# Two changes of order in an fp32 two-block transformer kernel: matmuls of rounded weights ahead of those of the remainders, and the next weights converted behind token tile 0's norm

## The chip, the core and the metric

The kernel runs on one core of one Trainium2 chip. The core has a matrix engine (TensorE, PE in the rows; its weight loads are listed apart as PEld), VectorE (DVE), ScalarE (ACT), GpSimd (POOL) and queues that start transfers (SyncE's is SP). The metric is the device time of one launch in microseconds, the median of several runs.

## The reference, cut to what matters

256 tokens of width 1024 pass through two transformer blocks. The first has stick-breaking attention beside a short convolution, then a gated feed-forward network with a convolution; the second has a gated delta rule (GDN) beside a forgetting attention (fox), then a squared-ReLU feed-forward network. Around them stand norms and residuals. At the end of the first block's mixing, and on into its feed-forward network, the reference reads:

```python
def rms_norm(x, g):
    xf = x.astype(jnp.float32)
    var = jnp.mean(xf * xf, axis=-1, keepdims=True)
    return (xf * lax.rsqrt(var + RMS_EPS) * g.astype(jnp.float32)).astype(x.dtype)
...
        x = x + rms_norm(merged @ w_out[l], norm_mix_post[l])

        h = rms_norm(x, norm_ffn_pre[l])
        u = causal_dwconv(h @ w_up[l], conv_ffn_w[l])
        a, g = jnp.split(u, 2, axis=-1)
        f = (jax.nn.gelu(g, approximate=True) * a) @ w_down[l]
        x = x + rms_norm(f, norm_ffn_post[l])
...
        hn = rmsnorm(h, norm_mlp_g[l])
        x = h + jnp.square(jax.nn.relu(hn @ w_up[l])) @ w_down[l]
```

All operands are fp32.

## The kernel before

**Products of split numbers.** A matrix product in fp32 is made of three products of rounded parts. A weight piece w (a `raw` tile of 512 KB, brought in by SP) is rounded by a cast on ScalarE to `wh`, and VectorE subtracts to get the remainder `wl`; this pair of instructions is `convert` of the class `Wt`, and stands in the trace at L183 and L184. Activations are split in the same way by `split` (cast on ScalarE, L122; subtraction on VectorE, L125). The raw tiles go round in 4 buffers, the `wh` tiles in 5 and the `wl` tiles in 4. The product is hi·hi + hi·lo + lo·hi.

**Two forms.** `mm_T` keeps weights in the array and moves activations: for each of 8 slices k of the contraction, `wh` meets [hi | lo] of 256 tokens (512 columns, L224), and then `wl` meets hi (256 columns, L225); 16 matmuls fill one tile `pT`. The text calls the two the wide and the narrow matmul. ScalarE and VectorE then read `pT`. `mm_N` keeps activations of one token tile (128 tokens, `tt` is 0 or 1) in the array and moves weights, always 512 columns (L261 to L263). Most projections go by `mm_T`; the output and down-projections (tiles `pN`) and the first projections of a stage go by `mm_N` (tiles `pM`).

**Transitions.** Between a projection that ends a stage and the next stage stand, for each token tile, `post_norm` (squares of the product on ScalarE, `fg` and `x` on VectorE), `norm` (two squares on ScalarE, the chain of small operations of `rsqrt` on VectorE, then `xm`), and `to_T` (eight transposes on TensorE into `tr`, then four splits). `normed` writes them for both tiles, with tile 0's transposes ahead of tile 1's norm. `head_N` (and `head_T`, which calls it) loads the first weights of the next stage, two `Wt` of four pieces each, and multiplies tile 0 by both, then tile 1. `down_tail` ends a projection: tile 0 finishes first, so that its norm runs beside tile 1's matmuls. There are four such places: in front of the first block's mixing (without `normed`), from the first output projection to the up-projection (near 195 us), from the down-projection to the second block (near 400 us), and from the second output projection to the last up-projection (near 745 us).

**What sets the order.** The code is written in one stream; a scheduler puts each engine's instructions in an order by its own estimate of when their inputs are there. Each engine works through its list strictly, and waits at its head.

Of the kernel before, what the change touches and what calls it, by code (L numbers as in the profile page):

```python
# [14 lines left out]
AF = mybir.ActivationFunctionType  # L15
ALU = mybir.AluOpType
AX = mybir.AxisListType

P = 128
T = 256  # L20
NT = T // P
D = 1024
KD = D // P
# [16 lines left out]
def two_blocks(ctx, tc, ins, out):  # L40
    nc = tc.nc
# [45 lines left out]
    mm = nc.tensor.matmul  # L87

    class Act:
# [3 lines left out]
        def __init__(self, s, n=KD, per=2, alloc=None):  # L93
            self.s, self.per, self.alloc, self.hl = s, per, alloc or t4, []
            for _ in range(0, n, per):
                self.more()
# [22 lines left out]

    def split(hi, lo, src, eng=None):  # L120
        if eng is None:
            nc.scalar.copy(hi, src)  # L122
        else:
            eng.tensor_copy(hi, src)
        nc.vector.tensor_sub(lo, src, hi)  # L125

    nc.scalar.preload_act_table_set("natural_log_exp_and_others")

# [31 lines left out]
    class Wt:  # L160


        def __init__(self, w, k0, n, c0, cols, alloc=None, later=False, raws=None):
            self.k0, self.per = k0, max(1, 1024 // cols)
            self.pieces, self.raw = [], []
            for k in range(k0, k0 + n, self.per):
                m = min(self.per, k0 + n - k)
                raw = wp.tile([P, m, cols], F32, tag="raw", name=nm("raw"), bufs=4) if raws is None else \
                    raws("raw", (P, m, cols))
                nc.sync.dma_start(raw, w[k * P:(k + m) * P, c0:c0 + cols].rearrange("(k p) c -> p k c", p=P))  # L170
                if alloc is None:
                    wh = wp.tile([P, m, cols], F32R, tag="wh", name=nm("wh"), bufs=5)
                    wl = wp.tile([P, m, cols], F32R, tag="wl", name=nm("wl"))
                else:
                    wh, wl = alloc("wh", (P, m, cols), F32R), alloc("wl", (P, m, cols), F32R)
                self.pieces.append((wh, wl))
                self.raw.append(raw)
                if not later:
                    self.convert()

        def convert(self):
# [36 lines left out]
    def mm_T(dst, wt, ct, kt, x):  # L218


        cs = slice(ct * P, (ct + 1) * P)
        for k in range(kt):
            wh, wl = wt.at(k, cs)
            mm(dst, wh, x.both(k), start=(k == 0), stop=False, skip_group_check=True)  # L224
            mm(dst[:, T:2 * T], wl, x.at(k)[0], start=False, stop=(k == kt - 1), skip_group_check=True)  # L225

    def proj_T(w, c0, ncols, x, dst=None):

# [46 lines left out]
    def tail_weights(w, k0, k1, alloc=None):  # L275
        return [Wt(w, k, 1, 0, D, alloc) for k in range(k0, k1)]

    def down_tail(banks, w, parts, wts, first):

        m = len(wts)  # L280
        wts = wts + tail_weights(w, parts[m][0], parts[-1][0] + 1)
        both = list(zip(wts, parts))
        for tt in range(NT):
            order = [(n, q) for q in both[:m] for n in range(2)] if tt == 0 else [(0, q) for q in both[:m]]
            order += [(0, q) for q in both[m:]]
            order += [(1, q) for q in (both[m:] if tt == 0 else both)]
            for n, (wt, (k, x, xk)) in order:
                mm_N(banks[tt][n], wt, k, x, xk, tt, slice(n * 512, (n + 1) * 512),
                     first and k == parts[0][0], k == parts[-1][0])

    def head_N(w, cols, x, ready, done):


        wts = [Wt(w, 0, KD, c, 512, a) for c, a in zip(cols, (tc4, None))]
        for tt in range(NT):
            ready(tt)
            for n in (0, 1) if tt == 0 else (1, 0):
                pt = pj("pM")
                for k in range(KD):
                    mm_N(pt, wts[n], k, x, k, tt, slice(None), k == 0, k == KD - 1)  # L300
                done(n, tt, pt)

    def head_T(w, cols, x, ready):

        nat = [t4("nat", (P, NT, 512)) for _ in cols]

        def done(n, tt, pt):
            nc.scalar.copy(nat[n][:, tt, :], pt)

        head_N(w, cols, x, ready, done)  # L310

        def pairs(t):
            for j in (0, 2):
                pt = pj("pT", (P, 2, T))
                for i in range(2):
                    for tt in range(NT):
                        nc.tensor.transpose(pt[:, i, tt * P:(tt + 1) * P], t[:, tt, (j + i) * P:(j + i + 1) * P], ident)
                yield j, pt

        return [pairs(t) for t in nat]  # L320


    def rsqrt(ss, scale, eps=EPS):


        v = nc.vector
        terms = ss if isinstance(ss, list) else [ss]
        shape = list(terms[0].shape)
        r, rc, q, y = tn("rsr", shape), tn("rsc", shape), tn("rsq", shape), tn("rsy", shape)
        for t in terms:  # L330
            a = tn("rsa", shape)
            if isinstance(eps, float):
                v.tensor_scalar(a, t, scale, eps, ALU.mult, ALU.add)
            else:
                v.scalar_tensor_tensor(a, t, scale, eps, ALU.mult, ALU.add)
            eps = a
        v.tensor_scalar(r.bitcast(I32), a.bitcast(I32), -0.5, float(0x5F300000), ALU.mult, ALU.add)
        v.tensor_mul(q, r, r)
        v.tensor_scalar(rc, r, -0.3985661334391346, None, ALU.mult)
        v.tensor_mul(y, q, a)  # L340
        v.scalar_tensor_tensor(q, y, -3.921194022600673, y, ALU.add, ALU.mult)
        v.scalar_tensor_tensor(q, q, 6.097508583838679, y, ALU.add, ALU.mult)
        v.scalar_tensor_tensor(r, q, -5.685303430259191, rc, ALU.add, ALU.mult)
        return r

    def norm(x, tt, g):

        s2 = tn("ss2", (P, 2))
        sq = t2("sq")
        for n in range(2):  # L350
            nc.scalar.activation(sq, x[tt][:, n * 512:(n + 1) * 512], AF.Square, accum_out=s2[:, n:n + 1])
        r = rsqrt([s2[:, 0:1], s2[:, 1:2]], 1.0 / D)
        xm = t4("xm", (P, D))
        for q in range(2):
            cs = slice(q * 512, (q + 1) * 512)
            gq = g[q] if isinstance(g, list) else g[:, cs]
            nc.vector.scalar_tensor_tensor(xm[:, cs], x[tt][:, cs], r, gq, ALU.mult, ALU.mult)
        return xm

    def to_T(dst, tt, xm, eng=None):  # L360

        for q in range(2):
            pt = pj("tr", (P, 4, P))
            for i in range(4):
                k = q * 4 + i
                nc.tensor.transpose(pt[:, i, :], xm[:, k * P:(k + 1) * P], ident)
            for i in (0, 2):
                split(*dst.at(q * 4 + i, slice(tt * P, (tt + 1) * P), 2), pt[:, i:i + 2, :], eng)

    def normed(x, g, dst, mid):  # L370

        xms = []
        for tt in range(NT):
            mid(tt)
            xms.append(norm(x, tt, g))
            if tt == 0:
                to_T(dst, 0, xms[0])
        return lambda tt: to_T(dst, tt, xms[tt]) if tt else None

    def post_norm(x, tt, banks, g):  # L380

# [14 lines left out]
    xr = [t4("x", (P, D)) for _ in range(NT)]  # L396
    nc.sync.dma_start(xr[0], x_in[0:P, :])
    g = t4("gain", (P, D))
# [5 lines left out]
            nc.sync.dma_start(xr[1], x_in[P:T, :])  # L404
    h = Act("hT")
    for tt in range(NT):
        to_T(h, tt, norm(xr, tt, g))
    for w in wv:
        w.convert()
    vN = t4("vN", (P, NT, ATT_W))  # L410
# [49 lines left out]
    pt = ps("pc")  # L460
    nc.tensor.transpose(pt[:, 0:g0 + 3], prow, ident[0:g0 + 3, 0:g0 + 3])
    nc.vector.tensor_copy(pcol, pt[:, 0:g0 + 3])
    pt = ps("fc")
# [107 lines left out]
    for j, pt in proj_T(w_in, CB, CONV_W, h):  # L571
        y = t2("cby", (P, 2, T))
# [36 lines left out]

    banks = proj_full_N(ins["w_out"][0], mh)  # L610
    ready = normed(xr, g_pre, h2, lambda tt: post_norm(xr, tt, banks[tt], g_post))


    w_up, w_down = ins["w_up"][0], ins["w_down"][0]
# [10 lines left out]
    banks = [[ps("pN"), ps("pN")] for _ in range(NT)]  # L625
    parts, first = [], True
# [20 lines left out]
    for (j, pa_), (_, pg_) in zip(*gens):  # L647
        if j >= 4:
            flush(NFH - 1)
        if j == NFH - 2:  # L650
            wts = tail_weights(w_down, NFH - TAIL, NFH - 4, tc4)
        y = []
        for part, pt in enumerate((pa_, pg_)):
            yy = t2("yy", (P, 2, T))
            for i in range(2):
                c = part * NFH + j + i
# [12 lines left out]
    ready = normed(xr, g_pre, u, lambda tt: post_norm(xr, tt, banks[tt], g_post))  # L669
# [493 lines left out]
    for j in range(0, KD, 2):  # L1163
        y = oTa[j // HG][:, j % HG:j % HG + 2, :]
# [4 lines left out]
    for j, pt in proj_T(ins["w_proj_gdn_2"][0], 0, D, ga):  # L1169
        y = t2("my", (P, 2, T))  # L1170
        nc.vector.scalar_tensor_tensor(y, sa[j // 4][:, j % 4:j % 4 + 2, :], 1.0, pt, ALU.add, ALU.mult)
        nc.vector.tensor_add(y, y, mb[j // 4][:, j % 4:j % 4 + 2, :])
        hi, lo = mh.at(j, n=2)
# [3 lines left out]
    hn = Act("hnT")  # L1177

    banks = proj_full_N(ins["w_out_2"][0], mh)

    xr = [t4("x", (P, D)) for _ in range(NT)]
# [8 lines left out]
    ready = normed(xr, g_mlp, hn, add_mix)  # L1190


    w_up, w_down = ins["w_up_2"][0], ins["w_down_2"][0]
    NK = D_FF_2 // P
    heads = head_T(w_up, (0, 512), hn, ready)
    head = chain(heads[0], ((4 + j, pt) for j, pt in heads[1]))
    gen = mix(head, (1, 3, 5, 7), 8, proj_T(w_up, 1024, D_FF_2 - 1024, hn))
    banks = [[ps("pN"), ps("pN")] for _ in range(NT)]
    parts, tails, first = [], [], True
    for j, pt in gen:  # L1200
# [6 lines left out]
        fh, o = ffn_act(j, NK - 1)  # L1207
        split(*fh.at(o, n=2), y)
        parts += [(j + i, fh, o + i) for i in range(2)]
    down_tail(banks, w_down, parts, wts, False)  # L1210
    for tt in range(NT):
        yo = t4("yo", (P, D))
        for n in range(2):
# [27 lines left out]
```

## Time and profile before

| | |
|---|---|
| median of 3 runs | 937.69 us (937.58 to 938.1) |
| the profiled execution | 936.81 us |
| its span, first to last instruction | 935.1 us |
| mean granted TensorE clock in it | 0.996 of 2.4 GHz |
| busy: TensorE, VectorE, ScalarE, GpSimd | 97%, 71%, 61%, 8% |

An engine's busy share is the share of the span in which at least one of its instructions runs. Matmuls overlap in the array, so a duration of one is longer than what it adds to the time; the distance between starts tells that. The granted clock is the share of full speed that the chip gave TensorE.

### The profile page before, as it was taken

How to read it: one execution, taken by the hardware profiler on the slowest of the kernel's cores; microseconds unless marked ns; L12 is line 12 of the kernel's file. 1: busy time of each engine (PE TensorE's matmuls, PEld its weight loads, DVE VectorE, ACT ScalarE, POOL GpSimd, SP SyncE). 2: the span in 40 equal slices, each digit the busy share in tenths (PEclk: the TensorE clock that was granted, in tenths of full speed). 3: DMA queues.
4: the chain of work that ended last, by engine and by line, in shares of the span. 5: the costliest groups of instructions: out<-in, count | busy, mean ns of one | idle time of the engine just before them, and what ended most of it. 6: DMA issues, size and time to landing. Idle time of an engine off the chain costs nothing.

```text
span 935.1 us, 13379 instructions
## 1 busy us (share of the span) xinstructions
PE 909.5 (97%) x4871; PEld 762.0 (81%) x4871; DVE 663.4 (71%) x1164; ACT 572.6 (61%) x987; POOL 74.9 (8%) x127
## 2 busy tenths in 40 slices
PE   5999999989999999999999999999999999999998
PEld 4887888768888888778888778888988778888886
DVE  6567657884888789867989878645688765555553
ACT  5567756554766666657867667754456456556561
POOL 4000000000000000000000089602000000000000
PEclk9999999989999999999999999999999999999999
DMA  7743456654564655564554354544346654556542
GB/s 252 227 139 113 130 186 226 203 180 139 180 201 159 208 174 199 197 210 128 163 160 128 100 157 145 159 136 138 100 135 226 222 181 159 187 176 198 181 151 99
DMA packets 118858, 157.87 MB, mean 169 GB/s; under 512 B 9813, under 2 KB 96072, under 8 KB 118792
## 3 DMA queue, kind: packets, MB, share of 16 engines
q1 hardware_dynamic: 117320, 153.08, 51.4%
q10 hardware_dynamic: 720, 2.62, 0.9%
q0 software_dynamic: 752, 1.31, 0.6%
q8 instruction: 38, 0.62, 0.3%
q14 instruction: 28, 0.23, 0.1%
HBM read 154.11 MB, written 2.88 MB: 168 GB/s over the span
## 4 chain that ended last, share of the span: by engine, by line
PE 81%; DVE 7%; DMA 6%; ACT 4%; issue 2%; SPq 0%; ACTq 0%; DVEq 0%
PE pT L224 30%; PE pT L225 15%; PE pN L262 5%; PE pN L261 5%; PE pN L263 5%; PE pM L261 4%; PE pM L263 4%; PE pM L262 3%; DVE wl L184 3%; DMA raw<-in_w_up_dram 2%; ACT wh L183 2%; PE pS L976 2%; DMA raw<-in_w_in_dram 1%; DMA raw<-in_w_down_dram 1%; DMA raw<-in_w_out_dram 1%
## 5 line engine op out<-in xcount | busy, mean ns | idle before, releaser
L184 DVE TENSOR_TENSOR wl<-raw,wh 128x1024 fp32r<-128x1024 f32 x282 | 345.2, 1230 | 70.2 <-PE pT L225 41.9
L183 ACT CAST wh<-raw 128x1024 fp32r<-128x1024 f32 x282 | 294.9, 1051 | 124.9 <-PE pT L224 57.1
L224 PE MATMUL pT<-uT,wh 128*128 128x512 f32 x384 | 139.4, 403 | 0.0
L225 PE MATMUL pT<-uT,wl 128*128 128x256 f32 x384 | 108.2, 282 | 0.0
L224 PE MATMUL pT<-hT,wh 128*128 128x512 f32 x288 | 102.4, 399 | 0.0
L224 PE MATMUL pT<-h2T,wh 128*128 128x512 f32 x288 | 101.8, 398 | 0.0
L237 DVE TENSOR_TENSOR py<-py,pT 128x256 f32<-128x256 f32 x136 | 56.2, 418 | 62.0 <-ACT py L236 61.3
L224 PEld LDWEIGHTS pT<-uT,wh 128*128 128x128 f32 x384 | 72.2, 188 | 16.1 <-issue 0.5
L261 PE MATMUL pN<-wh,fTh 128*128 128x512 f32 x216 | 84.1, 393 | 0.8 <-ACT wh L183 0.7
L236 ACT COPY py<-pT 128x256 f32<-128x256 f32 x136 | 49.3, 369 | 57.3 <-PE pT L225 57.0
L262 PE MATMUL pN<-wl,fTh 128*128 128x512 f32 x216 | 84.2, 391 | 0.1
L263 PE MATMUL pN<-wh,fTl 128*128 128x512 f32 x216 | 83.9, 390 | 0.0
L225 PE MATMUL pT<-hT,wl 128*128 128x256 f32 x288 | 80.8, 281 | 0.0
L225 PE MATMUL pT<-h2T,wl 128*128 128x256 f32 x288 | 80.8, 281 | 0.0
L225 PEld LDWEIGHTS pT<-uT,wl 128*128 128x128 f32 x384 | 72.5, 189 | 0.2
L224 PE MATMUL pT<-hnT,wh 128*128 128x512 f32 x192 | 68.2, 398 | 0.0
L224 PEld LDWEIGHTS pT<-hT,wh 128*128 128x128 f32 x288 | 54.0, 188 | 13.4 <-issue 0.2
L224 PEld LDWEIGHTS pT<-h2T,wh 128*128 128x128 f32 x288 | 54.1, 188 | 13.1
L225 PEld LDWEIGHTS pT<-h2T,wl 128*128 128x128 f32 x288 | 54.4, 189 | 0.2
L225 PEld LDWEIGHTS pT<-hT,wl 128*128 128x128 f32 x288 | 54.4, 189 | 0.0
L225 PE MATMUL pT<-hnT,wl 128*128 128x256 f32 x192 | 53.9, 281 | 0.0
L261 PEld LDWEIGHTS pN<-wh,fTh 128*128 128x128 f32 x216 | 40.5, 188 | 10.1 <-ACT wh L183 1.1
(375 smaller groups left out, 1684.6 us busy)
## 6 DMA issues: line engine op xcount, KB each, us to landing
raw<-in_w_in_dram SPq DMA_DIRECT2D x112, 512.0 KB, 4.2
raw<-in_w_up_dram SPq DMA_DIRECT2D x76, 512.0 KB, 4.5
raw<-in_w_down_dram SPq DMA_DIRECT2D x54, 512.0 KB, 4.1
raw<-in_w_out_dram SPq DMA_DIRECT2D x16, 512.0 KB, 3.5
raw<-in_w_proj_fox_dram SPq DMA_DIRECT2D x8, 512.0 KB, 3.6
raw<-in_w_proj_gdn_dram SPq DMA_DIRECT2D x8, 512.0 KB, 4.0
raw<-in_w_att_branch_dram SPq DMA_DIRECT2D x4, 512.0 KB, 3.3
raw<-in_w_conv_branch_dram SPq DMA_DIRECT2D x4, 512.0 KB, 4.2
```

Of the source, the lines that this page charges most:

```text
L183: nc.scalar.copy(wh, raw)
L184: nc.vector.tensor_sub(wl, raw, wh)
L224: mm(dst, wh, x.both(k), start=(k == 0), stop=False, skip_group_check=True)
L225: mm(dst[:, T:2 * T], wl, x.at(k)[0], start=False, stop=(k == kt - 1), skip_group_check=True)
L236: nc.scalar.copy(y[:, i, :], pt[:, 0:T])
L237: nc.vector.tensor_add(y[:, i, :], y[:, i, :], pt[:, T:2 * T])
L261: mm(dst, xh, wh, start=first, stop=False)
L262: mm(dst, xh, wl, start=False, stop=False)
L263: mm(dst, xl, wh, start=False, stop=last)
L976: mm(pt[:, hl, :], *f(hl), start=True, stop=True)
```

## The change

Four things are changed.

1. `mm_T` runs the eight matmuls of `wh` first and the eight of `wl` behind them, where they alternated.
2. In `head_N`, pieces of the next weights are converted only behind certain instructions of token tile 0: of the first `Wt` the pieces after the first `free` (2, at the last place 4) behind the second square and `xm` of tile 0's norm, of the second `Wt` all behind tile 0's last split. "Behind" (`issue_after`) sets a place in the engine's list; it adds no semaphore. `normed` passes these marks on.
3. `down_tail` ends both banks of tile 1 together, except at the last place, and orders tile 0's rest by bank.
4. `rsqrt` of a single column forms r·r·a in one operation where it took two.

```diff
@@ class Wt
-        def __init__(self, w, k0, n, c0, cols, alloc=None, later=False, raws=None):
+        def __init__(self, w, k0, n, c0, cols, alloc=None, later=False, raws=None, behind=None):
...
-                if not later:
+                if behind and len(self.pieces) > behind[0]:
+                    with tc.issue_after(behind[1]), tc.issue_after(behind[2]):
+                        self.convert()
+                elif not later:
                     self.convert()
@@ def mm_T
         for k in range(kt):
-            wh, wl = wt.at(k, cs)
-            mm(dst, wh, x.both(k), start=(k == 0), stop=False, skip_group_check=True)
-            mm(dst[:, T:2 * T], wl, x.at(k)[0], start=False, stop=(k == kt - 1), skip_group_check=True)
+            mm(dst, wt.at(k, cs)[0], x.both(k), start=(k == 0), stop=(k == kt - 1), skip_group_check=True)
+        for k in range(kt):
+            mm(dst[:, T:2 * T], wt.at(k, cs)[1], x.at(k)[0], start=False, stop=(k == kt - 1), skip_group_check=True)
@@ def down_tail
-    def down_tail(banks, w, parts, wts, first):
+    def down_tail(banks, w, parts, wts, first, last=False):
...
-            order = [(n, q) for q in both[:m] for n in range(2)] if tt == 0 else [(0, q) for q in both[:m]]
-            order += [(0, q) for q in both[m:]]
-            order += [(1, q) for q in (both[m:] if tt == 0 else both)]
+            if tt == 0:
+                order = [(n, q) for q in both[:m] for n in range(2)]
+                order += [(n, q) for n in range(2) for q in both[m:]]
+            elif last:
+                order = [(n, q) for n in range(2) for q in both]
+            else:
+                order = [(n, q) for q in both for n in range(2)]
@@ def head_N
-        wts = [Wt(w, 0, KD, c, 512, a) for c, a in zip(cols, (tc4, None))]
+        normed_, transposed = ready.marks
+        wts = [Wt(w, 0, KD, cols[0], 512, tc4, behind=(free, *normed_)),
+               Wt(w, 0, KD, cols[1], 512, None, behind=(0, *transposed))]
@@ def rsqrt
-        v.tensor_mul(q, r, r)
+        if shape[1:] == [1]:
+            v.scalar_tensor_tensor(y, r, a, r, ALU.mult, ALU.mult)
+        else:
+            v.tensor_mul(q, r, r)
+            v.tensor_mul(y, q, a)
         v.tensor_scalar(rc, r, -0.3985661334391346, None, ALU.mult)
-        v.tensor_mul(y, q, a)
@@ def norm
-        return xm
+        return xm, (act.ins, dve.ins)
@@ def normed
-        return lambda tt: to_T(dst, tt, xms[tt]) if tt else None
+        def ready(tt):
+            if tt:
+                to_T(dst, tt, xms[tt][0])
+
+        ready.marks = xms[0][1], split0
+        return ready
```

What it does to the lists of the engines, at the places that the prediction speaks of:

TensorE, the beginning of a tile `pT` of the first up-projection, before (the names are output, moving and stationary tile, with buffer numbers; line numbers are those of each program):

```order
L224 MATMUL pT_2187<-h2T_1732,wh_2176 128x512
L225 MATMUL pT_2187<-h2T_1732,wl_2177 128x256
L224 MATMUL pT_2187<-h2T_1732,wh_2176 128x512
L225 MATMUL pT_2187<-h2T_1732,wl_2177 128x256
```

and the whole tile with the change, where "x2" is two in a row:

```order
L226 MATMUL pT_2181<-h2T_1730,wh_2170 128x512 x2
L226 MATMUL pT_2181<-h2T_1731,wh_2170 128x512 x2
L226 MATMUL pT_2181<-h2T_1732,wh_2176 128x512 x2
L226 MATMUL pT_2181<-h2T_1733,wh_2176 128x512 x2
L228 MATMUL pT_2181<-h2T_1730,wl_2171 128x256 x2
L228 MATMUL pT_2181<-h2T_1731,wl_2171 128x256 x2
L228 MATMUL pT_2181<-h2T_1732,wl_2177 128x256 x2
L228 MATMUL pT_2181<-h2T_1733,wl_2177 128x256 x2
```

The alternation has become eight wide and eight narrow ones.

VectorE at the transition near 195 us, from tile 0's update of x to its xm, before (`x_95` is tile 0, `rsa` to `rsr` the chain of rsqrt):

```order
L391 SCALAR_TENSOR_TENSOR x_95<-fg_1886,rsr_1891,x_95 128x512 x2
L333 TENSOR_SCALAR rsa_1916<-ss_345_1908 128x1
L184 TENSOR_TENSOR wl_2011<-raw_2008,wh_2010 128x1024
L335 SCALAR_TENSOR_TENSOR rsa_1918<-ss_345_1908,rsa_1916 128x1
L184 TENSOR_TENSOR wl_2023<-raw_2020,wh_2022 128x1024
L337 TENSOR_SCALAR rsr_1912<-rsa_1918 128x1
L184 TENSOR_TENSOR wl_2017<-raw_2014,wh_2016 128x1024
L338 TENSOR_TENSOR rsq_1914<-rsr_1912 128x1
L339 TENSOR_SCALAR rsc_1913<-rsr_1912 128x1
L184 TENSOR_TENSOR wl_2029<-raw_2026,wh_2028 128x1024
L340 TENSOR_TENSOR rsy_1915<-rsq_1914,rsa_1918 128x1
```

and with the change, from the end of tile 0's chain to tile 1's (`x_96`), the splits and small operations between left out:

```order
L357 SCALAR_TENSOR_TENSOR rsr_1909<-rsq_1911,rsc_1910 128x1
L370 SCALAR_TENSOR_TENSOR xm_1923<-x_95,rsr_1909,gain_norm_ffn_pre_1464 128x512 x2
L187 TENSOR_TENSOR wl_2005<-raw_2002,wh_2004 128x1024
L187 TENSOR_TENSOR wl_2011<-raw_2008,wh_2010 128x1024
...
L412 SCALAR_TENSOR_TENSOR x_96<-fg_1946,rsr_1951,x_96 128x512 x2
L187 TENSOR_TENSOR wl_2017<-raw_2014,wh_2016 128x1024
L344 TENSOR_SCALAR rsa_1975<-ss_365_1967 128x1
L187 TENSOR_TENSOR wl_2023<-raw_2020,wh_2022 128x1024
L187 TENSOR_TENSOR wl_2029<-raw_2026,wh_2028 128x1024
L346 SCALAR_TENSOR_TENSOR rsa_1977<-ss_365_1967,rsa_1975 128x1
L187 TENSOR_TENSOR wl_2035<-raw_2032,wh_2034 128x1024
```

The four remainders have left tile 0's chain: two stand behind its xm, and the four of the second weights stand between tile 1's x and the rest of its chain.

ScalarE at the same place, before:

```order
L183 CAST wh_2022<-raw_2020 128x1024
L351 ACTIVATE sq_1909,ss_345_1908<-x_95 128x512
L183 CAST wh_2010<-raw_2008 128x1024
L351 ACTIVATE sq_1909,ss_345_1908<-x_95 128x512
L183 CAST wh_2016<-raw_2014 128x1024
```

and with the change:

```order
L365 ACTIVATE sq_1906,ss_345_1905<-x_95 128x512 x2
L186 CAST wh_2004<-raw_2002 128x1024
L186 CAST wh_2010<-raw_2008 128x1024
L407 ACTIVATE sq_1945,ss_356_1944<-pN_1736 128x512
L407 ACTIVATE sq_1945,ss_356_1944<-pN_1737 128x512
L122 CAST h2T_1730<-tr_1926 128x2x128
```

Tile 0's squares stand together, and the casts of its third and fourth piece come behind them.

## Rows read from the trace of the kernel before

**Rows 1.** The page, part 1: busy us (share of the span) xinstructions.

```profile
PE 909.5 (97%) x4871; PEld 762.0 (81%) x4871; DVE 663.4 (71%) x1164; ACT 572.6 (61%) x987; POOL 74.9 (8%) x127
```

**Rows 2.** The page, part 5: form xcount | busy, mean ns | idle before, releaser.

```profile
L184 DVE TENSOR_TENSOR wl<-raw,wh 128x1024 fp32r<-128x1024 f32 x282 | 345.2, 1230 | 70.2 <-PE pT L225 41.9
L183 ACT CAST wh<-raw 128x1024 fp32r<-128x1024 f32 x282 | 294.9, 1051 | 124.9 <-PE pT L224 57.1
```

**Rows 3.** Timeline of TensorE, two stretches of mm_T: start, duration, instruction.

```profile
226.83 0.39 PE L224 MATMUL pT<-h2T,wh 128*128 128x512 f32 x1
227.06 0.28 PE L225 MATMUL pT<-h2T,wl 128*128 128x256 f32 x1
...
249.09 0.40 PE L224 MATMUL pT<-h2T,wh 128*128 128x512 f32 x1
...
115.70 0.40 PE L224 MATMUL pT<-hT,wh 128*128 128x512 f32 x1
...
170.48 0.39 PE L224 MATMUL pT<-chT,wh 128*128 128x512 f32 x1
```

**Rows 4.** Timeline of TensorE, a run of mm_N, first and last.

```profile
916.57 0.39 PE L263 MATMUL pN<-wh,fTl 128*128 128x512 f32 x1
...
930.90 0.39 PE L263 MATMUL pN<-wh,fTl 128*128 128x512 f32 x1
```

**Rows 5.** Windows: stretch, length, busy per engine, PEclk, DMA share, GB/s.

```profile
194.57:200.00 5.43, 1.64 (x10) 0.84 (x8) 5.29 (x13) 2.34 (x5) 0.00 (x0) 1.00 0.87 280
200.00:207.00 7.00, 6.32 (x15) 4.96 (x16) 5.94 (x18) 3.22 (x9) 0.00 (x0) 0.51 0.71 231
```

**Rows 6.** Waits of TensorE: us in total, times, longest.

```profile
PE tr L366 <- POOL mtmp L131: 8.4, 1, 8.4
PE tr L366 <- DVE xm L357: 5.7, 2, 3.6
...
PE pM L263 <- DVE rsr L337: 0.5, 1, 0.5
```

**Rows 7.** Timeline of TensorE, 24 matmuls with 24-column weights, first and last.

```profile
418.33 0.28 PE L702 MATMUL pg<-uT,swh 128*24 128x256 f32 x1
...
420.99 0.28 PE L704 MATMUL pg<-uT,swl 128*24 128x256 f32 x1
```

**Rows 8.** Timeline of TensorE, four matmuls of one column, and the next.

```profile
470.82 0.61 PE L770 MATMUL pss<-ones,sq 128*128 128x1 f32 x4
471.28 0.48 PE L224 MATMUL pT<-uT,wh 128*128 128x512 f32 x1
```

**Rows 9.** Timeline of the weight loads, one in mm_T.

```profile
226.84 0.19 PEld L225 LDWEIGHTS pT<-h2T,wl 128*128 128x128 f32 x1
```

**Rows 10.** Timeline of ScalarE at the first transition.

```profile
191.05 1.03 ACT L183 CAST wh<-raw 128x1024 fp32r<-128x1024 f32 x1
```

**Rows 11.** Timeline of VectorE at the first transition (last row: tile 1).

```profile
189.74 0.75 DVE L391 SCALAR_TENSOR_TENSOR x<-fg,rsr,x 128x512 f32<-128x512 f32 x1
...
192.12 1.23 DVE L184 TENSOR_TENSOR wl<-raw,wh 128x1024 fp32r<-128x1024 f32 x1 [0.79 <-ACT wh L183]
...
197.70 1.42 DVE L357 SCALAR_TENSOR_TENSOR xm<-x,rsr,gain_norm_ffn_pre 128x512 f32<-128x512 f32 x2
...
209.83 1.42 DVE L357 SCALAR_TENSOR_TENSOR xm<-x,rsr,gain_norm_ffn_pre 128x512 f32<-128x512 f32 x2
```

**Rows 12.** Timeline of TensorE at the first transition, tile 0, then tile 1.

```profile
198.60 1.29 PE L366 MATMUL tr<-ident,xm 128*128 128x128 f32 x8 [3.65 <-DVE xm L357]
200.68 0.79 PE L261 MATMUL pM<-wh,h2T 128*128 128x512 f32 x1 [0.79 <-ACT h2T L122]
...
214.57 1.04 PE L366 MATMUL tr<-ident,xm 128*128 128x128 f32 x8
215.68 0.50 PE L261 MATMUL pM<-wh,h2T 128*128 128x512 f32 x1
```

**Rows 13.** Timeline of TensorE at the second transition, tile 1.

```profile
406.21 1.29 PE L366 MATMUL tr<-ident,xm 128*128 128x128 f32 x8 [2.09 <-DVE xm L357]
```

**Rows 14.** Timeline of ScalarE in the first block's attention: the exponential.

```profile
108.86 0.49 ACT L491 ACTIVATE la<-pz 128x384 f32<-128x384 f32 x1
```

**Rows 15.** Timeline of TensorE: the reader of that exponential.

```profile
114.46 0.65 PE L495 MATMUL pz<-la,vN 128*64 128x256 f32 x2
```

More of the change, by code (lines that the diff above doesn't have):

```diff
@@ L121, in split @@
         if eng is None:
-            nc.scalar.copy(hi, src)
+            act = nc.scalar.copy(hi, src)
         else:
-            eng.tensor_copy(hi, src)
-        nc.vector.tensor_sub(lo, src, hi)
+            act = eng.tensor_copy(hi, src)
+        return act.ins, nc.vector.tensor_sub(lo, src, hi).ins
     nc.scalar.preload_act_table_set("natural_log_exp_and_others")
@@ L289, in down_tail, with head_N @@
                      first and k == parts[0][0], k == parts[-1][0])
-    def head_N(w, cols, x, ready, done):
-        wts = [Wt(w, 0, KD, c, 512, a) for c, a in zip(cols, (tc4, None))]
+    def head_N(w, cols, x, ready, done, free=2):
+        normed_, transposed = ready.marks
+        wts = [Wt(w, 0, KD, cols[0], 512, tc4, behind=(free, *normed_)),
+               Wt(w, 0, KD, cols[1], 512, None, behind=(0, *transposed))]
         for tt in range(NT):
@@ L301, in head_N, with head_T @@
                 done(n, tt, pt)
-    def head_T(w, cols, x, ready):
+    def head_T(w, cols, x, ready, free=2):
         nat = [t4("nat", (P, NT, 512)) for _ in cols]
@@ L308, in done @@
             nc.scalar.copy(nat[n][:, tt, :], pt)
-        head_N(w, cols, x, ready, done)
+        head_N(w, cols, x, ready, done, free)
         def pairs(t):
@@ L350, in norm @@
         for n in range(2):
-            nc.scalar.activation(sq, x[tt][:, n * 512:(n + 1) * 512], AF.Square, accum_out=s2[:, n:n + 1])
+            act = nc.scalar.activation(sq, x[tt][:, n * 512:(n + 1) * 512], AF.Square, accum_out=s2[:, n:n + 1])
         r = rsqrt([s2[:, 0:1], s2[:, 1:2]], 1.0 / D)
@@ L355, in norm @@
             cs = slice(q * 512, (q + 1) * 512)
-            gq = g[q] if isinstance(g, list) else g[:, cs]
-            nc.vector.scalar_tensor_tensor(xm[:, cs], x[tt][:, cs], r, gq, ALU.mult, ALU.mult)
-        return xm
+            dve = nc.vector.scalar_tensor_tensor(xm[:, cs], x[tt][:, cs], r, g[:, cs], ALU.mult, ALU.mult)
+        return xm, (act.ins, dve.ins)
     def to_T(dst, tt, xm, eng=None):
@@ L367, in to_T @@
             for i in (0, 2):
-                split(*dst.at(q * 4 + i, slice(tt * P, (tt + 1) * P), 2), pt[:, i:i + 2, :], eng)
+                last = split(*dst.at(q * 4 + i, slice(tt * P, (tt + 1) * P), 2), pt[:, i:i + 2, :], eng)
+        return last
     def normed(x, g, dst, mid):
@@ L376, in normed @@
             if tt == 0:
-                to_T(dst, 0, xms[0])
-        return lambda tt: to_T(dst, tt, xms[tt]) if tt else None
+                split0 = to_T(dst, 0, xms[0][0])
+        def ready(tt):
[3 more added lines that the diff above has]
+        return ready
     def post_norm(x, tt, banks, g):
@@ L406, in two_blocks @@
     for tt in range(NT):
-        to_T(h, tt, norm(xr, tt, g))
+        to_T(h, tt, norm(xr, tt, g)[0])
     for w in wv:
@@ L1194, in two_blocks @@
     NK = D_FF_2 // P
-    heads = head_T(w_up, (0, 512), hn, ready)
+    heads = head_T(w_up, (0, 512), hn, ready, 4)
     head = chain(heads[0], ((4 + j, pt) for j, pt in heads[1]))
@@ L1209, in two_blocks @@
         parts += [(j + i, fh, o + i) for i in range(2)]
-    down_tail(banks, w_down, parts, wts, False)
+    down_tail(banks, w_down, parts, wts, False, True)
     for tt in range(NT):
```

## Prediction

> **What bounds the kernel now.** The page's first part comes first: TensorE is busy 97% of the span, VectorE 71%, ScalarE 61% [rows 1]. So the time is TensorE's: the slots of its instructions, plus the few places where it stands still or runs at its lower clock. Among the costliest groups the conversions of weights matter here, 1.05 us on ScalarE and 1.23 us on VectorE each [rows 2]. The durations that this part gives for matmuls are those of pipelined ones; what a matmul costs is the distance from its start to the next start, so the timeline of starts is the view to read.
>
> In a long stretch of mm_T, 63 pairs start in 22.26 us, 353 ns a pair, some 236 of it from a wide matmul (512 columns) to the narrow one (256) behind it and 117 from the narrow to the next wide; in another, 158 pairs take 54.78 us, 347 each, 230 and 117 [rows 3]. In a run of mm_N, where only 512-column matmuls follow each other, 63 steps take 14.33 us, 227.5 each [rows 4]. The same columns cost up to 8.5 ns more with a narrow one behind them.
>
> The windows by stage show where TensorE stands still: between 194.57 and 200 us it is busy 1.64 of 5.43 us, and from 200 to 207 the granted clock is 0.51, the 1.2 GHz level [rows 5]. That is the transition from the first output projection to the first up-projection. The list of waits says how little else there is: after 8.4 us for POOL mtmp, in a part that the change doesn't touch, the longest entry is 5.7 us in two waits of the transposes for xm [rows 6].
>
> **The change, part by part.** *Regrouping in mm_T.* The 1344 pairs stand in 168 groups of eight (a few are two of four). Each group now has seven steps wide to wide, one wide to narrow, seven narrow to narrow and one narrow to wide. Three of these have rows: 227.5, 230 to 236, 117. Narrow behind narrow with 128-column weights has none. The nearest by columns is a run of 24 matmuls of 256 columns whose weights have 24 columns: 23 steps in 2.66 us, 115.7 each [rows 7]. The nearest by weights is four matmuls of one column with 128-column weights: 0.46 us to the next start, 115 each [rows 8]. The load of a narrow matmul's weights starts at 226.84, 10 ns behind the start of the wide one before it (226.83) [rows 3, 9]. So a load runs beside the matmul ahead of it, and fits behind 256 columns, but only just. I take 117, the row of today's narrow matmul with the right weights. Most stretches have 353, so I take 352 for the mean pair, as 235 + 117. A group then costs 7x227.5 + 235 + 8x117 = 2764 ns against 8x352 = 2816: 52 ns less, times 168 = **8.7 us**. The ends: narrow steps of 115 (7x2 ns more per group, 2.4 us) and 1 to 2 ns a pair for the reading of stretches, 13 us; and nothing, if the surplus moves along to the narrow steps (124.5 each).
>
> [...]
>
> *Conversions at the first transition.* Now: x is updated from 189.74 on VectorE; between the two squares of its norm ScalarE casts a weight [rows 10]; and among the small operations of rsqrt VectorE makes four remainders, the first at 192.12, so that xm comes at 197.70 [rows 11]. The transposes follow at 198.60 after 3.65 us of idle, the first matmul at 200.68 [rows 12]. With the change the squares stand together, and no remainder stands between x and xm (the rows of the order are shown under the change). x ends at 190.5; the second square and its read-out, some 0.7 us, make 191.2; six small operations of 0.19 us, 192.4; xm then. The transposes could start 0.9 us behind xm's start (as 198.60 behind 197.70), at 193.3. The out-projection's last matmul starts at 194.57, so they follow it at 194.8. From the transposes to the first matmul I take 1.7 us (2.08 now, with a cast of 1.05 ahead of the split): 196.5, 4.2 us earlier. The idle ahead of the clock's fall is gone, and with it the loss at 1.2 GHz: 15 matmuls in 6.32 us [rows 5], 0.42 each against 0.227, 2.9 us.
>
> Not all of that is kept. The third and fourth remainder of the first weights come behind xm (1.4 us), done at about 195.0 and 196.2; the first two pieces give TensorE 12 matmuls, 2.7 us from 196.5, so these are in time (0.3 us charged). The second weights' four come behind tile 0's last split and so ahead of tile 1's xm. VectorE has, from 196.2: splits (4x0.38), a chain (7x0.19), fg (2x0.64), x (1.4), four remainders (4x1.2), and of a second chain five operations behind the last of them (1.0): 196.2 + 1.5 + 1.3 + 1.3 + 1.4 + 4.8 + 1.0 = 207.5, and 0.4 for waits between splits, 207.9 for xm. It is now at 209.83, with the transposes at 214.57 and tile 1's first matmul at 215.68, held by TensorE's own work [rows 11, 12]. In the new order TensorE comes to them at 196.5 + 48x0.2277 + 0.3 = 207.7, and gets them at 207.9 + 0.9 = 208.8. Tile 1's first matmul is then at 209.7 to 209.9 instead of 215.68: **6.0 us**. Ends: 7.0 (nothing late) and 4.0 (transfers of the second weights late by 2 us, since raw buffers come free later when their casts wait).
>
> *The second transition* waits 2.09 us for tile 1's xm [rows 13], with three remainders ahead of the x that leads to it. These still stand ahead of it, but a cast of a late raw now comes between the two squares, and the pieces of the first weights leave tile 0's chain. I take 0.6 gained; ends 0.9 gained and 1.0 lost. *The last transition* has one wait of 0.5 for a small operation behind remainders [rows 6]: 0.4, ends 0 and 0.6.
>
> *down_tail.* Both banks of tile 1 now end together; the square and fg of its first bank lose their head start. Tile 0's head, 10.9 us of matmuls, hides it; without that cover it is a square and fg, 1.3 us, already within the 207.9.
>
> *rsqrt and tables.* Twelve VectorE operations fewer, 0.19 us each; those in the norms are counted above. On ScalarE an exponential moves behind a sigmoid, with two more table loads (1.28 us each); it is now at 108.86 and comes some 3.2 us later, its reader on TensorE stands at 114.46 [rows 14, 15], so about 2 us of slack hide it. Without cover: 2.6 us.
>
> Sum: 8.7 + 6.0 + 0.6 + 0.4 = 15.7 us off the profiled execution's 936.81 (span 935.1 and 1.7 around it), 921.1. That execution lies 0.88 below the median of the runs, 937.69; added back, **922.0 us**.
>
> **Rivals.** *A. Regrouping gives nothing:* narrow behind narrow costs 124.5. For it: a load takes 115 of today's 117, nothing to spare. Against: 115.7 with small weights. Time 937.7 - 7.0 = 930.7.
>
> *B. The first transition gives little:* the second weights' remainders hold tile 1's norm until TensorE stands still as long as now, and the clock falls behind tile 1 instead of tile 0. For it: 4.8 us of remainders move exactly there. Against: TensorE's own 10.9 us. Time 937.7 - 8.7 - 1 = 928.
>
> *C. Slower:* the load of a narrow matmul's weights isn't hidden behind another narrow one. If load and matmul add up, 115 + 117 = 232 a step: 168x7x115 ns = 135 us more, 1066 with the transitions' gain. It decides as soon as the 1176 steps eat 15.7 us: 13 ns each, narrow at 130. Against: today's narrow to wide step holds a full load in 117. For: no row has two of them in a row.
>
> *D. No change:* A and B together, 936.7.
>
> **How the numbers follow.** My forecast (both work) 0.62, A 0.16, B 0.11, C 0.06, D 0.05. Its own range is 916 (13 + 7.0 + 0.9 + 0.6 = 21.5 off) to 929. To leave out no more than 2 in 10 the range takes in B, and A with the transition's poor end (4.0: 933.7): **916 to 934**. About 0.2% (2 us) is what a measurement here can tell from none. Faster by more: forecast, A and B, 0.89; within it: D, 0.05; slower: C, 0.06.
>
> **What would show it.** Right: starts at 115 to 118 in a narrow run and 227 to 228 in a wide one; transposes at 194.8; full clock from 200 to 207; tile 1's transposes near 208.8; no new wait of TensorE over 1 us. (These times of before shift by some 3 us where regrouping has acted ahead of them.) Wrong: narrow steps of 124 or more; tile 1's xm more than 14 us behind tile 0's transposes; a wait for wl or wh in the first 24 matmuls behind the transposes; TensorE waiting for the moved exponential.

## The result, and the profile after

| | before | after |
|---|---|---|
| median of 5 runs | 937.58 us | 929.71 us |
| ratio of the runs, 95% interval | | 0.9907 (0.9888 to 0.9926) |
| profiled execution, its span | 936.81, 935.1 us | 929.96, 928.2 us |

The kernel became 7.9 us faster by the medians (8.7 by the ratio), about half of the 15.7 us that were forecast, and the time lies inside the range. The page's first part, after:

```profile
PE 907.0 (98%) x4871; PEld 764.0 (82%) x4871; DVE 657.0 (71%) x1152; ACT 570.9 (62%) x989; POOL 73.3 (8%) x127
```

Against [rows 1] only the 12 VectorE operations and two ScalarE table loads differ in number. The timeline of TensorE in a stretch of mm_T, where a row with "x8" is a run of eight:

```profile
892.51 2.00 PE L226 MATMUL pT<-hnT,wh 128*128 128x512 f32 x8
894.36 1.11 PE L228 MATMUL pT<-hnT,wl 128*128 128x256 f32 x8
895.31 0.40 PE L226 MATMUL pT<-hnT,wh 128*128 128x512 f32 x1
```

From start to start, eight wide steps take 1.85 us, 231 each, and eight narrow ones 0.95, 119 each; a pair is 350 ns, where [rows 3] have 353 in most stretches and 347 in others. Over all groups of the trace the steps within a run are 230.6 wide and 119.0 narrow. The timeline of TensorE at the first transition, tile 0 and then tile 1:

```profile
199.14 1.03 PE L379 MATMUL tr<-ident,xm 128*128 128x128 f32 x8
200.40 0.50 PE L264 MATMUL pM<-wh,h2T 128*128 128x512 f32 x1 [0.23 <-ACT h2T L122]
...
211.83 1.22 PE L379 MATMUL tr<-ident,xm 128*128 128x128 f32 x8
```

The stall of 3.65 us ahead of the transposes [rows 12] is gone, and tile 1's transposes follow 12.7 us behind tile 0's instead of 16. But the transition comes late. The branch projections ahead of it take 23.8 us up to the output projection (149.46 to 173.28), where before they took 22.2 (148.64 to 170.83). The timeline of TensorE in the output projection that follows them:

```profile
176.68 0.50 PE L264 MATMUL pN<-wh,mT 128*128 128x512 f32 x1 [0.50 <-ACT wh L186]
178.60 0.50 PE L265 MATMUL pN<-wl,mT 128*128 128x512 f32 x1 [1.41 <-DVE wl L187]
```

and the windows by stage (columns as in [rows 5]):

```profile
180.00:194.00 14.00, 14.00 (x57) 11.37 (x56) 11.80 (x21) 6.12 (x10) 0.00 (x0) 0.88 0.82 281
194.00:200.00 6.00, 6.00 (x32) 4.99 (x30) 5.09 (x13) 4.49 (x11) 0.00 (x0) 1.00 0.05 18
200.00:207.00 7.00, 6.71 (x29) 5.02 (x28) 6.82 (x20) 5.62 (x11) 0.00 (x0) 1.00 0.48 152
```

The clock is full from 200 to 207, where it was 0.51. In this execution it fell instead behind the two waits, near 180 us, for half as long (0.88 over 14 us against 0.51 over 7).

### The profile page after: what moved, and what is told of

It reads as the page before. It is cut to its first block, busy times and chain, and to the rows that moved or that the text cites. A ratio compares the mean times of both kernels' runs of the same rounds, so it can differ in the third digit from the quotient of the medians.

```text
span 928.2 us, 13339 instructions
## 1 busy us (share of the span) xinstructions
PE 907.0 (98%) x4871; PEld 764.0 (82%) x4871; DVE 657.0 (71%) x1152; ACT 570.9 (62%) x989; POOL 73.3 (8%) x127
## 4 chain that ended last, share of the span: by engine, by line
PE 84%; DVE 7%; DMA 4%; ACT 3%; issue 1%; SPq 0%; ACTq 0%; DVEq 0%
PE pT L226 30%; PE pT L228 15%; PE pN L264 6%; PE pN L265 6%; PE pN L266 6%; PE pM L264 4%; PE pM L265 4%; PE pM L266 4%; DVE wl L187 3%; PE pS L997 2%; DMA raw<-in_w_out_dram 1%; ACT wh L186 1%; DMA raw<-in_w_in_dram 1%; DMA raw<-in_w_proj_gdn_dram 1%; DMA raw<-in_w_down_dram 1%
## 5 line engine op out<-in xcount | busy, mean ns | idle before, releaser
L226 PE MATMUL pT<-uT,wh 128*128 128x512 f32 x384 | 102.3, 403 | 0.0
L226 PE MATMUL pT<-hT,wh 128*128 128x512 f32 x288 | 73.4, 396 | 0.0
L226 PE MATMUL pT<-h2T,wh 128*128 128x512 f32 x288 | 72.2, 392 | 0.0
L226 PEld LDWEIGHTS pT<-hT,wh 128*128 128x128 f32 x288 | 51.6, 188 | 10.4 <-issue 0.2
L228 PEld LDWEIGHTS pT<-uT,wl 128*128 128x128 f32 x384 | 52.2, 190 | 3.6
L228 PE MATMUL pT<-uT,wl 128*128 128x256 f32 x384 | 53.8, 282 | 0.0
L226 PE MATMUL pT<-hnT,wh 128*128 128x512 f32 x192 | 47.8, 391 | 0.0
L265 PEld LDWEIGHTS pN<-wl,fTh 128*128 128x128 f32 x216 | 40.6, 188 | 8.6 <-DVE wl L187 0.8
L266 PEld LDWEIGHTS pN<-wh,fTl 128*128 128x128 f32 x216 | 40.6, 188 | 8.4
L228 PEld LDWEIGHTS pT<-hT,wl 128*128 128x128 f32 x288 | 39.3, 190 | 2.8
L228 PEld LDWEIGHTS pT<-h2T,wl 128*128 128x128 f32 x288 | 39.3, 190 | 2.8
```

Source lines behind the costliest of these rows:

```text
L226: mm(dst, wt.at(k, cs)[0], x.both(k), start=(k == 0), stop=(k == kt - 1), skip_group_check=True)
L228: mm(dst[:, T:2 * T], wt.at(k, cs)[1], x.at(k)[0], start=False, stop=(k == kt - 1), skip_group_check=True)
L265: mm(dst, xh, wl, start=False, stop=False)
L266: mm(dst, xl, wh, start=False, stop=last)
```

## The experiments

Ratios are to the kernel before on the same chip, with 95% intervals; 1% is 9.4 us.

**e1: everything but the regrouping.** In the changed kernel mm_T alternates again:

```diff
         for k in range(kt):
-            mm(dst, wt.at(k, cs)[0], x.both(k), start=(k == 0), stop=(k == kt - 1), skip_group_check=True)
-        for k in range(kt):
-            mm(dst[:, T:2 * T], wt.at(k, cs)[1], x.at(k)[0], start=False, stop=(k == kt - 1), skip_group_check=True)
+            wh, wl = wt.at(k, cs)
+            mm(dst, wh, x.both(k), start=(k == 0), stop=False, skip_group_check=True)
+            mm(dst[:, T:2 * T], wl, x.at(k)[0], start=False, stop=(k == kt - 1), skip_group_check=True)
```

> The changed kernel with the wide and narrow matmuls of mm_T alternating again; the conversions behind tile 0, down_tail and rsqrt as changed. Theory (regrouping pays, but about 20 ns a group: narrow steps of 119 to 120 and slower wide steps behind them, 3.3 us in all, and it costs about 2.4 us of new waits in the branch and output projections): 929.7 + 3.3 - 2.4 = 930.6 us, with the first matmul of the output projection near 170.5 and no wait of 1.4 us in it. Rival (those waits come from the new order of conversions, not from regrouping): 933, with the waits still there. Second rival (regrouping costs on balance): under 929.

Measured: 0.9889 (0.9871 to 0.9907), 10.4 us faster than before: the conversions, banks and rsqrt give all of the gain. The second rival holds as far as it says that regrouping doesn't pay on balance. The theory had the output projection right (it starts at 170.31), but a wait of 1.08 us for wl stays in it, as before (1.0). The timeline of TensorE at the first transition in e1:

```profile
194.01 1.03 PE L379 MATMUL tr<-ident,xm 128*128 128x128 f32 x8
195.27 0.50 PE L264 MATMUL pM<-wh,h2T 128*128 128x512 f32 x1 [0.22 <-ACT h2T L122]
196.40 0.50 PE L266 MATMUL pM<-wh,h2T 128*128 128x512 f32 x1 [0.40 <-DVE h2T L125]
207.00 1.26 PE L379 MATMUL tr<-ident,xm 128*128 128x128 f32 x8
```

and the windows: the whole kernel behind its start runs at full clock.

```profile
12.30:920.00 907.70, 900.17 (x4854) 756.29 (x4853) 655.37 (x1131) 565.06 (x974) 63.88 (x88) 1.00 0.56 170
```

**e2: the regrouping alone,** on the kernel before (the same lines the other way round).

> The kernel before with only mm_T regrouped. Theory: 937.6 - 3.3 + 2.4 = 936.7 us; the stall of 3.6 us ahead of the transposes of the first transition and the lower clock behind it stay. Rival (the new waits near 175 us belong to the conversions): 934.3. If regrouping were worth the 8.7 us of the prediction: 929.

Measured: 0.9997 (0.9985 to 1.0009): nothing. The steps are as in the changed kernel (230.7 and 119.0 in the mean). Where part of them went is in the list of waits of TensorE in e2:

```profile
PE tr L366 <- DVE xm L357: 6.7, 2, 4.5
PE pN L261 <- ACT mT L1174: 2.0, 1, 2.0
PE pN L262 <- DVE wl L184: 1.9, 3, 1.3
...
PE pT L223 <- DVE py L237: 0.4, 1, 0.4
```

The transposes' waits for xm were 5.7 us [rows 6]; those for mT and for wl in the output projections were 0.9 and 1.3, and the last entry wasn't in the list. These four are 3.1 us more together; other entries fell, and the whole list, without the 8.4 us at the kernel's start, went from 12.9 to 15.5 us. TensorE comes to its next operand earlier, and waits there for the other engines. The steps gain 3.4 us (20 ns in 168 groups, worked out from the means above), so waits take most of it; in two executions of the changed kernel (after and e5) the same sum differs by 1.1 us, so it is no closer than that. The theory's 936.7 us lies inside the interval; both 934.3 and 929 are out.

**e3: sixteen and sixteen.** Both output tiles of a weight pair at once:

```diff
-                pt = pj("pT")
-                mm_T(pt, wt, i, kt, x)
+            pts = [pj("pT"), pj("pT")]
+            for lo in range(2):
+                for i in range(2):
+                    mm_T(pts[i], wt, i, kt, x, lo)
```

> The changed kernel with the two output tiles of a weight pair taken together: sixteen wide matmuls, then sixteen narrow ones. Theory (the wide steps are slow, 231 to 235, only in the first six behind a narrow run, and 226.7 from there): this start is paid once for two groups, so the wide mean falls from 230.6 to about 228.8, 2.2 us less: 927.5 us. Rival (the slow wide steps pay back what the narrow run left behind, so twice as many are slow behind a run twice as long): 929.7, the wide mean unchanged.

Measured: 0.9945 (0.9925 to 0.9964), slower than by eights (0.9900 in e5). The wide mean did fall, to 228.7 ns, so slow wide steps belong to the start of a run; but the narrow mean rose to 120.1, and TensorE waited elsewhere (1.83 us in the branch projections, up to 153.71 us, and 0.9 to 1.2 at several other places). The expectation of the time fell, that of the steps held.

**e4: half the columns.** The narrow matmul on tile 0's 128 tokens only; the other half of that product is left out.

```diff
-            mm(dst[:, T:2 * T], wt.at(k, cs)[1], x.at(k)[0], start=False, stop=(k == kt - 1), skip_group_check=True)
+            mm(dst[:, T:T + P], wt.at(k, cs)[1], x.at(k, slice(0, P))[0], start=False, stop=(k == kt - 1), skip_group_check=True)
```

> The changed kernel with the narrow matmuls cut to 128 columns (tile 0's tokens alone get the product of remainder weights; the rest of that product is left out). Theory (a narrow step of 119 to 120 is the load of 128 weight columns, not the 256 columns): the step stays at 110 to 120 and the time falls by at most 10 us. Rival (the columns set it): steps near 65 ns, and 1344 x 55 ns = 74 us less.

Measured: 968.81 us in one run, slower, which no theory had. The timeline of TensorE, two groups:

```profile
279.77 2.08 PE L226 MATMUL pT<-h2T,wh 128*128 128x512 f32 x8
281.69 1.00 PE L228 MATMUL pT<-h2T,wl 128*128 128x128 f32 x8
282.53 2.07 PE L226 MATMUL pT<-h2T,wh 128*128 128x512 f32 x8
284.43 1.00 PE L228 MATMUL pT<-h2T,wl 128*128 128x128 f32 x8
```

With half the columns a narrow step is 105 in the mean, not 65: the first of each run takes some 60, the others 111 to 114. In these runs the loads start 111 to 112 ns apart, and each matmul starts some 59 ns behind the start of its own load; so here the pace is that of the loads of 128 weight columns, near the 115 that rival A gave a load. It is below the 119 to 120 of the changed kernel, so the columns count there too. The wide steps behind rise to 240 in the mean of eight, the first of them to some 283. The time itself went into waits (5.7 us for an operand of the GDN part, 5.3 and 3.9 in the output projections) and into lower clock (0.86 from 430 to 480 us); why the waits became so long was not followed up.

**e5, e6, e7: the changed kernel again, and its parts.** e6 is e1 with the old order of down_tail, e7 is e6 with the old rsqrt, that is, the conversions behind tile 0 alone.

> The changed kernel itself, on the same chip as the next three. Theory (regrouping gives nothing by itself and costs where it makes the first transition's neighbours wait): ratio to before 0.990, above those of the kernels with alternating matmuls by 0.001 to 0.003. Rival (regrouping pays its 3 us of shorter steps): below them by 0.003.

> Alternating matmuls, conversions behind tile 0 and rsqrt as changed, the order of down_tail as before. Theory (tile 0's head hides the order of the banks): the ratio to before stays at 0.989, as with the changed order. Rival (the changed order is what lets tile 1's update come in time, or delays it): 1 to 2 us to either side, seen at tile 1's transposes of the first two transitions.

> The kernel before with the conversions behind tile 0 as the only change. Theory (nearly all of the gain is there): ratio 0.989 to 0.990, 9 to 10 us; rsqrt's twelve operations give at most 0.6 us of it. Rival (rsqrt or the banks carry part of it): above 0.992.

Measured: e5 0.9900 (0.9884 to 0.9917), e6 0.9900 (0.9883 to 0.9916), e7 0.9928 (0.9911 to 0.9945). e5 and e6 are equal, so in the changed kernel regrouping shows neither the cost that e5's theory gave it nor the gain of its rival. The order of the banks makes no difference that can be told (e1 against e6: 0.9889 and 0.9900), as e6's theory said. About seven tenths of the gain are the conversions' own, less than e7's theory had; its rival, above 0.992, came. rsqrt comes out at 2.6 us, with intervals that just overlap, more than its operations cost: in e7 the second transition still has its stall. The timeline of TensorE there, in e7 and then in e6, which differs by rsqrt alone:

```profile
400.33 1.29 PE L372 MATMUL tr<-ident,xm 128*128 128x128 f32 x8 [2.25 <-DVE xm L363]
```

```profile
397.77 1.29 PE L375 MATMUL tr<-ident,xm 128*128 128x128 f32 x8 [1.20 <-DVE xm L366]
```

VectorE's list there shows why: with the old rsqrt the scheduler put four remainders between tile 1's fg and its x, with the new one three. That the shorter chain moves that place, and not the operations' time, is the difference of the two lists. Behind the longer stall the clock falls in e7 and not in e6 (windows as in [rows 5], e7 first):

```profile
400.00:406.00 6.00, 5.64 (x21) 4.49 (x22) 3.70 (x8) 2.44 (x5) 0.00 (x0) 0.72 0.24 94
```

```profile
400.00:406.00 6.00, 6.00 (x28) 4.95 (x27) 5.39 (x6) 4.84 (x6) 0.00 (x0) 1.00 0.55 136
```

From the first down-projection matmul to these transposes e7 takes 1.5 us more than e6 (157.3 and 155.8), and the 12 us of work behind them 1.6 more. The runs agree: five of e7 have a mean granted clock of 0.996 to 0.998 and took 932.3 to 934.2 us; the sixth, at 1.000, took 930.17.

The clock of e5 in the stretch where the first execution of the changed kernel lost it:

```profile
177.18 0.50 PE L265 MATMUL pN<-wl,mT 128*128 128x512 f32 x1 [1.42 <-DVE wl L187]
```

```profile
180.00:194.00 14.00, 13.73 (x61) 10.98 (x60) 11.20 (x22) 7.28 (x14) 0.00 (x0) 1.00 0.82 262
```

**e8, e9, e11: by twos and by fours.** Two wide, two narrow matmuls in turn; e8 with the other changes, e9 on the kernel before, e11 by fours with the other changes.

```diff
+        for k0 in range(0, kt, 2):
+            for k in (k0, k0 + 1):
+                mm(dst, wt.at(k, cs)[0], x.both(k), start=(k == 0), stop=False, skip_group_check=True)
+            for k in (k0, k0 + 1):
+                mm(dst[:, T:2 * T], wt.at(k, cs)[1], x.at(k)[0], start=False, stop=(k == kt - 1), skip_group_check=True)
```

> Alternating by twos: two wide, two narrow matmuls, and so on; conversions, banks and rsqrt as changed. Theory (a narrow step behind a wide one takes 113, the next 119, then 120, and wide steps behind narrow ones 227 to 236): two pairs take 227 + 235 + 113 + 119 = 694 ns, 347 a pair against 352 alternating, 6 us less over 1344 pairs, of which waits elsewhere eat at least half: ratio 0.986. Rival (the slow wide steps come behind each narrow run whatever its length): 235 + 235 + 113 + 119 = 702, 351 a pair, ratio 0.989 as alternating.

> The kernel before with mm_T alternating by twos as the only change. Theory (by twos and by eights have the same mean pace, 349.5 ns a pair; by eights the gain is eaten by waits of TensorE for late operands, by twos not): ratio 0.996 to 0.998, 2 to 3 us, where by eights it was 0.9997. Rival (the pace of mm_T is worth nothing in any order, and twos gained only together with the conversions): 1.000.

> Alternating matmuls by fours, conversions, banks and rsqrt as changed. Theory (pace as by twos and by eights, waits between them): ratio 0.986 to 0.988, TensorE's waits in the branch and output projections between the two. Rival (only twos keep the operands in time): 0.990 as by eights.

Measured: e8 0.9851 (0.9832 to 0.9870), e9 0.9965 (0.9953 to 0.9978), e11 0.9871 (0.9855 to 0.9886). The timeline of TensorE in e8:

```profile
890.92 0.63 PE L227 MATMUL pT<-hnT,wh 128*128 128x512 f32 x2
891.39 0.39 PE L229 MATMUL pT<-hnT,wl 128*128 128x256 f32 x2
...
893.02 0.62 PE L227 MATMUL pT<-hnT,wh 128*128 128x512 f32 x2
```

Six pairs in 2.10 us are 350 each, the pace by eights, not the 347 expected; the ratios of all three theories held. At the same pace, twos give 3.3 us alone and 4.6 us over the changed kernel on the same chip (0.9851 against 0.9900), where eights give nothing. So the difference between them lies outside the steps of mm_T. Some 1.6 us of it lie in one stage: from the first branch projection to the output projection it is 22.2 us before, 22.3 in e9 and 23.9 in e2. The lists of waits hold 0.7 us (14.8 in e9 and 15.5 in e2, without the kernel's start). That a group of eight makes waits because it wants all its wh within 1.85 us is argued, not shown, and the groups of the branch projections are of four. By fours (e11) can't be told from twos. e8 beats both kernels, by 14 us the one before.

**e10: half the weights.** By eights, narrow matmuls on 64 of the 128 weight columns; the remainder product of half of the output channels is left out.

> The changed kernel, by eights, with the narrow matmuls on 64 of the 128 weight columns (the remainder product of half of the output channels is left out). Theory (a narrow step of 120 waits for the load of its 128 weight columns, and the slow wide steps of 229 to 236 behind a narrow run come from the backlog of loads): narrow steps at 113 to 116, as with 24-column weights, and wide steps at 227 throughout; a group 7x227 + 227 + 8x115 = 2736, 58 ns less, up to 10 us less in all, less what waits eat. Rival (the columns of the moving side set 120, or the slow wide steps have another cause): narrow steps stay at 119 to 120, or wide steps at 230.6 in the mean.

Measured: 924.24 us in one run. The timeline of TensorE:

```profile
886.02 2.00 PE L226 MATMUL pT<-hnT,wh 128*128 128x512 f32 x8
887.86 1.08 PE L228 MATMUL pT<-hnT,wl 128*64 128x256 f32 x8
888.77 0.40 PE L226 MATMUL pT<-hnT,wh 128*128 128x512 f32 x1
```

Narrow steps fall to 114 with half the weight columns, as they fall to 111 to 114 with half the moving ones (e4). So neither the load nor the columns alone make 119 to 120; how the two add up to it stays open. The wide steps stay at 230: the second half of the theory fell, the narrow matmuls' loads aren't what slows them.

**e12: the first weights only.** e1 with the second weights' pieces converted as early as before:

```diff
-               Wt(w, 0, KD, cols[1], 512, None, behind=(0, *transposed))]
+               Wt(w, 0, KD, cols[1], 512, None)]
```

> Alternating matmuls, banks and rsqrt as changed, but only the first weights' pieces are converted behind tile 0; the second weights' as early as before. Two of their remainders then stand between tile 0's x and xm again (2.4 us). Theory (tile 0's xm was ready 2.2 us ahead of the end of the output projection when both stood behind, 191.8 to 194.0, so the stall comes back only in part): transposes 1 to 2 us later than with both, ratio 0.990 to 0.992, full clock. Rival (it is the second weights that make the gain): a stall of over 3 us and the lower clock behind it, ratio above 0.995.

Measured: 0.9968 (0.9958 to 0.9978). At the first transition the theory held: the transposes start at 195.87 instead of 194.01, at full clock, behind a wait of 1.13. The ratio came from a place that no theory had, the last transition. The timeline of TensorE there:

```profile
746.13 0.80 PE L264 MATMUL pM<-wh,hnT 128*128 128x512 f32 x1 [4.31 <-ACT hnT L122]
```

and that of ScalarE:

```profile
742.78 1.04 ACT L186 CAST wh<-raw 128x1024 fp32r<-128x1024 f32 x1 [1.64 <-DMA raw<-in_w_up_dram]
744.76 1.04 ACT L186 CAST wh<-raw 128x1024 fp32r<-128x1024 f32 x1 [0.94 <-DMA raw<-in_w_up_dram]
```

The split of tile 0 stands in ScalarE's list behind casts that wait for transfers; TensorE waits for it 4.31 us, and the clock falls (0.72 from 740 to 752). From the second output projection to mm_T of the last up-projection it is 53.7 us, 47.3 in e1. The rival's ratio came, but not by the stall that it named.

## Why the prediction was half right

**Regrouping: the sum's first term was mis-sized, and its cover missing.** It took 117 for narrow behind narrow and 227.5 for wide behind wide, 52 ns a group; measured are 119.0 and 230.6, 20 ns a group, 3.4 us in all for the 8.7. The narrow step is more than its load or its columns ask for alone (111 to 114 each, e4 and e10); and the first five wide steps behind a narrow run are slow. The row of [rows 4] is of a run of 63, too far from a run of eight. Then even these 3.4 us were taken as time. In e2 the list of waits grew by 2.6: TensorE is busy 97%, but at those places another engine ends last. That is rival A, with 930.7 us for 929.71, though its cause (all of the surplus moves to the narrow steps) is right for part only. That its figure comes so near is in part luck: in e1 the three transitions gave 9.4 us, where the sum had 7.0, and in the changed kernel the branch and output projections gave some of it back.

The Trainium skill, page "TensorE: Matmul & The Clock Gate", section "Back-to-back issue gap", gives columns over 2.4 GHz plus 2.5 ns as the gap of an isolated matmul; as an estimate from it, that is 109.2 and 215.8 here. The Trainium skill adds there that in a stream of loads and matmuls both set the spacing. The steps here, 119.0 and 230.6, agree with the second statement (e4 and e10 for the narrow ones) and lie above the formula's figures.

**First transition: right, a little more than forecast.** From the first branch projection (148.64 us before, 148.13 in e1) to the first matmul of the down-projection (249.43 and 241.83) e1 is 7.1 us shorter against the 6.0 forecast, just above the upper end given, the clock included; e7, with the conversions alone, is 6.4 shorter. Transposes at 194.01 and tile 1's at 207.00 (forecast 194.8 and 208.8); xm of tile 1 starts at 206.06 (207.9). The remainders that moved ahead of tile 1's norm are, as forecast, covered by TensorE's own work. Rival B is out. In the changed kernel itself part of this is lost ahead of it, in the branch and output projections. Two waits grew past 1 us, both in output projections (1.41 from 1.0, and 1.15 from 0.9).

**Second and last transition: right in sign, the second for another reason.** In e1 the stretch between the first down-projection matmul and tile 1's transposes of the second transition is 1.35 us shorter (forecast 0.6), that from the second output projection to mm_T of the last up-projection 0.97 (0.4). With the conversions alone (e7) the last is 1.4 shorter, but the second 0.5 longer, and its wait is 2.25 us, where it was 2.09 [rows 13]. So the gain at the second isn't that of the pieces that leave tile 0's chain, as forecast, but comes with rsqrt.

**rsqrt: the step that counted operations failed.** It moved the list of VectorE by a remainder, and the clock with it (e7), and so counts for more than their 0.19 us each. **down_tail and tables: as forecast.** There is no difference from the banks that the intervals can tell, and no wait for the moved exponential in the list of waits.

## What to carry to other kernels

A busy share of 97% doesn't say that a shorter step shortens the kernel: look at which waits follow the stretch, and whether what they wait for comes from TensorE. Small groups can have the pace of large ones and lose less around them (twos against eights here); that this is a matter of deadlines for operands is not shown. Where engines work through lists strictly, what matters of a conversion is who stands behind it, above all when it waits for a transfer. A few small operations fewer can move a long one to another place in such a list, and be worth more, or less, than their own time.

## What the hardware showed unexpectedly

In a run, a narrow matmul with 128 weight columns costs 119 to 120 ns when it moves 256 columns and still 111 to 114 when it moves 128; with 64 weight columns and 256 moved it costs 113 to 114. Loads and matmuls overlap: in e4 a matmul starts some 59 ns behind the start of its load, while the loads start 111 to 112 ns apart. Wide matmuls behind a narrow run are slow for about five steps (233, 236, 228, 232, 231 ns, then 227) with small weights too; the cause stays open, as does why alternating pairs run at 353 ns in some stretches and 347 in others, mostly in the same stretches in the alternating kernels. And the clock fell behind different stalls in traces of different kernels: behind waits of 0.50 and 1.41 us in the changed kernel, where e5, the same program with waits of 0.39 and 1.42, kept it full; and behind 2.25 us in e7, but not behind 2.09 in the kernel before.
